# Weight-block sums of the convolution's quads: on VectorE while they are used, or in DRAM beforehand

## The chip, the cores and the metric

One core of one Trainium2 chip runs the whole program. The metric is the device time of one execution in microseconds, taken as the median of several runs. Beside these there is one profiled execution, whose span and instruction times are what the views of the profile show.

## What is computed

A trunk of two layers on a sequence of 512 tokens with 1024 features, all in float32. Cut to what matters here:

```python
def short_conv_mixer(x, w_in, w_conv, w_out):     # w_in: 1024 x 3072
    proj = x @ w_in
    bgate, cgate, xh = jnp.split(proj, 3, axis=-1)
    u = cgate * xh
    conv = causal_depthwise_conv(u, w_conv)       # width 3
    return (bgate * conv) @ w_out

def sqrelu_mlp(x, w_up, w_down):                  # 1024 -> 4096 -> 1024
    h = jax.nn.relu(x @ w_up)
    return (h * h) @ w_down

for i in range(2):
    x = x + rms_norm(mixer_i(rms_norm(x)))        # i = 0: mLSTM, i = 1: short_conv_mixer
    x = x + rms_norm(sqrelu_mlp(rms_norm(x)))
```

So the order of the work is mLSTM mixer, first MLP, convolution mixer, second MLP.

## The kernel before, in words

**Matmuls.** Float32 products are made from float32r halves: `split` (L79 to L84) writes the rounded half with a cast on ScalarE (ACT, L80) and the rest with a subtraction on VectorE (DVE, L81), and `mm3` (L112 to L117) issues three matmuls on TensorE (PE) for each pair of operands.

**Quads.** The products with `w_up` and with the convolution's `w_in` are made in pieces called quads. A quad takes two column blocks of 256 columns of the weights, so with the two halves of the 1024 rows it has four weight blocks of 512 x 256: a and b in the upper half, c and d in the lower one. In place of eight block products it makes seven, by the Strassen-Winograd scheme: each of the seven multiplies one combination of weight blocks by one combination of activation blocks. The activation side (`a11`, `a12`, `a22`, `p1`, `n2`, `r3`, `p4`) is made once for each layer in the class `Seven` (L199). The weight side is a, c, d and four sums: a+b, b+d, a+b+d and a+b+c+d. Before the change each quad loads its four blocks and makes the four sums with `tensor_tensor` additions on DVE. `Quad.block` (L814) is a load of 512 KB into a buffer called `raw` on the SyncE queue (SP), `Quad.factor` (L823) is the split of one weight operand, `prod` (L793) is one of the seven products, 24 matmuls of 256 columns.

**Three ways through a quad.** `enter` (L935) begins the first three quads of a layer early (products with a and c), while the layer before ends, and has the first quad's four sums made by `sums` (L849, additions on L852, L855, L856, L858). `run_first` (L861) finishes quad 0. `run` (L887) does the others; its four additions are L899, L905, L920 and L931. The convolution has six quads: four that give the gated value (`gated`, L1025) and two for the output gate (`out_gate`, L1064), run in the order 0, 1, 3, 2, 4, 5 (L1078 to L1080). Each MLP has eight.

**Buffers.** `raw` has 7 buffers, `u` (split weights, activations, residual) 15, the PSUM tiles `pu` 4 and `pd` 2. A load on SP waits until its `raw` buffer is released, that is, until the last DVE instruction that reads the buffer's former tile. In the convolution the value `u` of each gated quad takes a `raw` buffer as well, from a memset on GpSimd (POOL, L1036) to the last L1053.

**The end of a layer.** `last_product` (L280) makes the product with the last 1024 rows of `w_down`, or the whole product with `w_out`: two row tiles at a time in the two `pd` banks. `done` (L303) reads a finished bank with ACT (L181) and with DVE (L315 after a mixer, L318 after an MLP), and the next product in that bank waits for them. POOL makes a small power (L173) for each norm and, after an MLP, the product with the gain (L321). Between the last products `ahead` starts the next layer's `enter`.

**Queues.** SP carries all weight loads, in program order. POOL's queue carries the saving of the residual (`xd<-u`, L785), its loading again (`u<-xd`, L776, from `fetch_x`), gains (L160), the powers and the memsets, in program order too. A scheduler sets the order on each engine from the program and its own costs. In the first MLP each of the quads 2 to 7 is preceded by `down(g)` (L979), the product with one eighth of `w_down`; its results are added to `ys` by DVE (L1004, for g = 0 copied by ACT, L1002).

Of the kernel before, what the change touches and what calls it, by code (L numbers as in the profile page):

```python
# [8 lines left out]
F32 = mybir.dt.float32  # L9
# [5 lines left out]
P = 128  # L15
# [24 lines left out]
def tile_hybrid_trunk(  # L40
# [239 lines left out]
    def last_product(wm, r0, hT, g, tail, accs=None, ends=False, ahead=None):  # L280
# [61 lines left out]
        for t in range(2, NT):  # L342
            if ahead is not None:
                ahead()
            for cs in parts[t]:
                o = pd()
                ks(o, t, cs, 0, KO)
                done(o, t, cs)

# [404 lines left out]

    def scores_and_core(t):
        scores(t)
        if t > 0:
            core(t - 1, 0)
# [47 lines left out]
    class Quad:  # L806
# [3 lines left out]
        def __init__(self, wm, c0, c1, xT, take, claim=lambda: None):  # L810
            self.wm, self.cols, self.xT, self.take = wm, (c0, c1), xT, take
            self.claim = claim

# [47 lines left out]
        def run_first(self):  # L861
# [5 lines left out]
            f4, f5, f6, f7, f3 = (self.factor(t) for t in self.ts)  # L867
# [19 lines left out]
        def run(self, begun):  # L887
# [4 lines left out]
            bank = pd if begun else pu  # L892
            self.claim()
            a, b = self.block(0, 0), self.block(0, 1)
            if not begun:
                self.f1 = self.factor(a)
                self.begin(pu)
            y = self.y
            tt(out=a, in0=a, in1=b, op=ALU.add)  # L899
            f5 = self.factor(a)  # L900
# [3 lines left out]
            d = self.block(1, 1)  # L904
            tt(out=a, in0=a, in1=d, op=ALU.add)  # L905
            f6 = self.factor(a)
# [8 lines left out]
            c = self.block(1, 0)  # L915
# [4 lines left out]
            tt(out=b, in0=b, in1=d, op=ALU.add)  # L920
            prod(y, self.factor(b), f["r3"], False)
            o = bank()
            nc.scalar.mul(by_tile(o), by_tile(y), -1.0)
            prod(z, self.factor(d), f["p4"], False)
# [6 lines left out]
            tt(out=a, in0=a, in1=c, op=ALU.add)  # L931
            prod(o, self.factor(a), f["a22"], False)
            self.take(0, 1, self.values(), by_tile(o))

    def enter(quads):  # L935
# [7 lines left out]
        quads[0].sums()  # L943
# [12 lines left out]
    def mlp(i, xT, gain_of, tail_of, ends=False, ahead=None):  # L956
# [4 lines left out]
        def quad(g):  # L961
# [13 lines left out]
            return Quad(w_up[i], g * 512, g * 512 + 256, xT, take)  # L975
# [3 lines left out]
        def down(g):  # L979
            if g == 0:  # L980
                ys.extend(token_tiles())
            for hf, cs in enumerate(halves()):
# [6 lines left out]
                for t in range(NT):  # L989
# [11 lines left out]
                    if g == 0:  # L1001
                        nc.scalar.copy(yh, o)  # L1002
                    else:
                        nc.vector.tensor_tensor(out=yh, in0=yh, in1=o, op=ALU.add)  # L1004

# [13 lines left out]
    def conv(xT, gain_of, tail_of, ahead):  # L1019
# [5 lines left out]
        def gated(p):  # L1025
# [36 lines left out]
            return Quad(wm, D + p * 256, 2 * D + p * 256, xT, take, claim)  # L1062

        def out_gate(b):  # L1064
# [8 lines left out]
            return Quad(wm, b * 512, b * 512 + 256, xT, take)  # L1073
# [54 lines left out]
```

## Time and profile before

| | |
|---|---|
| median of 3 runs | 1108.53 us (1106.28 to 1109.0) |
| the profiled execution: its time | 1111.46 us |
| its span | 1109.7 us |
| its mean granted TensorE clock | 0.994 |
| first MLP, steady part, PE time | about 283 to 531 us |
| convolution, quads, PE time | 578.7 to 706.7 us |
| convolution, last product, PE time | 706.7 to 741.5 us |

How to read the views. The page gives the busy time of each engine over the span. The view of stretches gives, for each stretch of time, the busy time of each engine with its number of instructions, the granted TensorE clock as a share, the busy share of the 16 DMA engines and what they moved. Matmuls are pipelined and their ends are modelled, so PE can look busy while it runs below its rate; matmuls per microsecond say more. The view of waits gives for an engine and a line what it waited for, the sum in us, how often, and the longest. The view of groups gives count, busy time and mean duration of instructions of one line, then the idle time before them. The timeline gives start, duration, engine, line, operands and, in brackets, idle time before an instruction and what ended it. The DMA view gives packets and busy share of each queue, and for each kind of transfer its size and the median time from issue to landing.

### The profile page before, as it was taken

To read this page: it belongs to the slowest core of one execution; us is meant where nothing else is said; L and a number is where in the kernel's file an instruction comes from. 1 tells how busy PE (TensorE), PEld (TensorE's weight loads), DVE (VectorE), ACT (ScalarE), POOL (GpSimd) and SP (SyncE) were. 2 spreads that over 40 slices of the span, in tenths; PEclk is the share of its full clock that TensorE was granted. 3 is DMA by queue.
4 is the path that set the end of the run, shared out by engine and by line. 5 is a ranking of instruction groups with operands and counts; after the bars stand their busy time and mean duration, and the time that the engine had idled before them with its cause. 6 is when DMAs were issued, how large, how long until landed. Compare 5 with 4: busy or idle time off the path is not lost. (4 is left out here: it accounts for less than half of the span.)

```text
span 1109.7 us, 16027 instructions
## 1 busy us (share of the span) xinstructions
PE 1080.6 (97%) x6531; PEld 951.8 (86%) x6531; DVE 758.5 (68%) x1008; ACT 503.8 (45%) x780; POOL 70.3 (6%) x114
## 2 busy tenths in 40 slices
PE   7999999999999999999999999899999999999997
PEld 5878887789899899899879999778989989989986
DVE  5561567489776775758579998848967667575843
ACT  6441445365554244335346545636554434424521
POOL 1100010110000000000231000011000000000011
PEclk9999999999999999999999999989999999999999
DMA  8420264136344133163424362623533413415201
GB/s 266 134 76 1 76 228 138 71 102 198 117 135 134 46 126 125 47 208 110 144 89 153 95 209 96 200 105 104 182 117 128 135 56 114 133 44 203 96 19 57
DMA packets 104783, 133.73 MB, mean 121 GB/s; under 512 B 5221, under 2 KB 76165, under 8 KB 104710
## 3 DMA queue, kind: packets, MB, share of 16 engines
q1 hardware_dynamic: 100246, 116.46, 33.3%
q0 software_dynamic: 4464, 16.25, 4.0%
q8 instruction: 51, 0.84, 0.3%
q14 instruction: 22, 0.18, 0.1%
HBM read 124.31 MB, written 8.39 MB: 120 GB/s over the span
## 5 line engine op out<-in xcount | busy, mean ns | idle before, releaser
L81 DVE TENSOR_TENSOR u<-raw,u 128x1024 fp32r<-128x1024 f32 (+1 forms) x270 | 320.5, 1200 | 123.5 <-ACT u L80 123.1
L80 ACT CAST u<-raw 128x1024 fp32r<-128x1024 f32 (+1 forms) x270 | 272.3, 1028 | 216.2 <-PE pd L117 159.3
L115 PE MATMUL pu<-u 128*128 128x256 f32 (+1 forms) x1112 | 337.2, 303 | 3.5 <-ACT u L80 3.4
L116 PE MATMUL pu<-u 128*128 128x256 f32 (+1 forms) x1112 | 335.6, 302 | 0.8 <-DVE u L81 0.8
L117 PE MATMUL pu<-u 128*128 128x256 f32 (+1 forms) x1112 | 334.7, 301 | 0.8 <-DVE u L81 0.8
L115 PE MATMUL pd<-u,hb 128*128 128x512 f32 (+1 forms) x648 | 256.1, 395 | 5.5 <-DVE t L315 4.4
L116 PE MATMUL pd<-u,hb 128*128 128x512 f32 (+1 forms) x648 | 255.2, 394 | 0.0
L117 PE MATMUL pd<-u,hb 128*128 128x512 f32 (+1 forms) x648 | 255.1, 394 | 0.0
L115 PEld LDWEIGHTS pu<-u 128*128 128x128 f32 x1112 | 210.6, 189 | 13.7 <-ACT u L80 4.8
L116 PEld LDWEIGHTS pu<-u 128*128 128x128 f32 x1112 | 210.4, 189 | 10.1 <-DVE u L81 1.6
L117 PEld LDWEIGHTS pu<-u 128*128 128x128 f32 x1112 | 210.5, 189 | 9.6 <-DVE u L81 1.3
L115 PEld LDWEIGHTS pd<-u,hb 128*128 128x128 f32 x648 | 122.4, 189 | 35.2 <-DVE t L315 5.3
L117 PEld LDWEIGHTS pd<-u,hb 128*128 128x128 f32 x648 | 122.3, 189 | 28.2
L116 PEld LDWEIGHTS pd<-u,hb 128*128 128x128 f32 x648 | 122.5, 189 | 27.9 <-DVE u L81 0.6
L115 PE MATMUL pd<-u 128*128 128x256 f32 x312 | 88.3, 283 | 4.1 <-ACT pu L840 2.4
L116 PE MATMUL pd<-u 128*128 128x256 f32 x312 | 87.5, 281 | 0.0
L117 PE MATMUL pd<-u 128*128 128x256 f32 x312 | 87.3, 281 | 0.0
L1004 DVE TENSOR_TENSOR u<-u,pd 128x512 f32<-128x512 f32 x80 | 54.6, 683 | 36.8 <-PE pd L117 36.5
L181 ACT ACTIVATE junk<-u 128x512 bf16<-128x512 f32 (+1 forms) x49 | 30.5, 622 | 74.1 <-DVE u L318 53.3
L80 ACT CAST hb<-t 128x512 fp32r<-128x512 f32 x80 | 48.9, 619 | 32.5 <-DVE t L968 26.7
L115 PEld LDWEIGHTS pd<-u 128*128 128x128 f32 x312 | 58.8, 188 | 5.2 <-ACT pu L840 2.8
L116 PEld LDWEIGHTS pd<-u 128*128 128x128 f32 x312 | 58.8, 188 | 0.0
(173 smaller groups left out, 851.7 us busy)
## 6 DMA issues: line engine op xcount, KB each, us to landing
raw<-in_w_mlp_up_dram SPq DMA_DIRECT2D x76, 512.0 KB, 4.5
raw<-in_w_mlp_down_dram SPq DMA_DIRECT2D x64, 512.0 KB, 4.2
raw<-in_w_in_conv_dram SPq DMA_DIRECT2D x30, 512.0 KB, 4.8
raw<-in_w_in_mlstm_dram SPq DMA_DIRECT2D x24, 512.0 KB, 4.7
xd<-u POOLq DMA_DIRECT2D x12, 512.0 KB, 3.0
u<-xd POOLq DMA_DIRECT2D x12, 512.0 KB, 5.8
raw<-in_w_out_mlstm_dram SPq DMA_DIRECT2D x8, 512.0 KB, 4.1
raw<-in_w_out_conv_dram SPq DMA_DIRECT2D x8, 512.0 KB, 4.6
```

The lines of the kernel that those rows point to most:

```text
L80: hi = nc.scalar.copy(dst_hi, src)
L81: lo = nc.vector.tensor_tensor(out=dst_lo, in0=src, in1=dst_hi.bitcast(F32), op=ALU.subtract)
L115: nc.tensor.matmul(o, lh, rh, start=first, stop=False, skip_group_check=True)
L116: nc.tensor.matmul(o, lh, rl, start=False, stop=False, skip_group_check=True)
L117: nc.tensor.matmul(o, ll, rh, start=False, stop=last, skip_group_check=True)
L181: nc.scalar.activation(junk(n), src, AF.Square, scale=float(D) ** -0.5, accum_out=ms[:, i : i + 1])
L1004: nc.vector.tensor_tensor(out=yh, in0=yh, in1=o, op=ALU.add)
```

## The change

The four sums of all six quads of the convolution are made in DRAM during the first MLP. Two DRAM tensors hold them: `cx` for the four gated quads (four sums, 512 x 1024 each: the four quads' 256 columns lie side by side), `og` for the two output-gate quads (four sums, 512 x 2 x 256 each). A part is a range of rows of one tensor: four parts of 128 rows of `cx`, two of 256 rows of `og`, so that each transfer of a part has 512 KB. A part is nine transfers from POOL's queue. The first writes four elements from the tile `yh` that the MLP has just written, which only sets the part's place in time. Four plain copies fill the four sums with a, b, d and c. Then come four adding transfers: b onto the first sum, d onto the second, the first sum onto the third, the third onto the fourth. The third waits for the first, the fourth for the third. A part is recorded at the end of the first column half of each `down(g)`, g = 0 to 5, of the first MLP.

In the convolution each operand is now loaded as it stands, a sum by `sum_block`, a block by `block`: seven loads a quad, where there were four (six for a quad that is begun early). The additions on DVE go: 20 in the five `run` quads, 4 in `sums`. The MLPs are as before.

```diff
+    class Sums:
+        def __init__(self, name, wm, c0, c1, shape, key, quads):
+            self.all = dram.tile([4, 512] + shape, F32, name=name)
...
+            self.blocks = src(0, c0), src(0, c1), src(1, c0), src(1, c1)
...
+        def make(self, r0, r1, mark):
+            a, b, c, d = (blk[r0:r1] for blk in self.blocks)
+            f = [self.all[n, r0:r1] for n in range(4)]
+            first = self.all[:, r0]
+            first = first[:, 0, 0:1] if len(first.shape) > 2 else first[:, 0:1]
+            nc.gpsimd.dma_start(first, mark)
+            for dst, blk in zip(f, (a, b, d, c)):
+                nc.gpsimd.dma_start(dst, blk)
+            for dst, blk in list(zip(f, (b, d))) + [(f[2], f[0]), (f[3], f[2])]:
+                nc.gpsimd.dma_start(dst, blk, accum_op=ALU.add, max_dma_last_dim=D)
...
+    cx = Sums("cx", wc, D, 2 * D, [D], "conv", [D + p * 256 for p in range(4)])
+    og = Sums("og", wc, 0, 256, [2, 256], "conv", [0, 512])
+    later = [(cx, p * P, (p + 1) * P) for p in range(4)] + [(og, 0, 256), (og, 256, 512)]
...
+        def sum_block(self, i):
+            raw = raw_tile([4, 256])
+            nc.sync.dma_start(raw, self.pre[i])
+            return raw
...
-            f4, f5, f6, f7, f3 = (self.factor(t) for t in self.ts)
+            if self.pre is None:
+                f4, f5, f6, f7, f3 = (self.factor(t) for t in self.ts)
+            else:
+                f4, f5, f6, f7 = (self.factor(self.sum_block(i)) for i in (3, 0, 2, 1))
+                f3 = self.factor(self.block(1, 1))
...
-            tt(out=a, in0=a, in1=b, op=ALU.add)
-            f5 = self.factor(a)
+            if not pre:
+                tt(out=a, in0=a, in1=b, op=ALU.add)
+            f5 = self.factor(self.sum_block(0) if pre else a)
...
-        quads[0].sums()
+        if quads[0].pre is None:
+            quads[0].sums()
...
+                if i == 0 and hf == 0 and later:
+                    sm, r0, r1 = later.pop(0)
+                    sm.make(r0, r1, yh[0:4, 0:1])
```

Three places show what this does to the order. The first is POOL's queue during the first MLP. Before, from the last gain of the mLSTM layer's end to the first MLP's last product, it holds only the four loads of the residual (`xd` is the residual in DRAM, `u` its place in SBUF):

```order
L160 DMA gain<-in_norm_g_dram 128x1024
L776 DMA u<-xd_1452 128x1024
L776 DMA u<-xd_1453 128x1024
L776 DMA u<-xd_1454 128x1024
L776 DMA u<-xd_1455 128x1024
L321 TENSOR_TENSOR u<-u,gain 128x512 x3
```

Now, the fourth part of `cx`, the first of `og`, the residual's loads, and the beginning of the last part:

```order
L379 DMA cx<-u 4x1
L381 DMA cx<-in_w_in_conv_dram 128x1024 x4
L383 DMA cx<-in_w_in_conv_dram 128x4x256 x2
L383 DMA cx<-cx 512x256 x2
L379 DMA og<-u 4x1
L381 DMA og<-in_w_in_conv_dram 512x1x256 x4
L383 DMA og<-in_w_in_conv_dram 512x1x256 x2
L383 DMA og<-og 512x256 x2
L818 DMA u<-xd_1454 128x1024
L818 DMA u<-xd_1455 128x1024
L818 DMA u<-xd_1456 128x1024
L818 DMA u<-xd_1457 128x1024
```

Fifty-four transfers now stand between that gain and the L321 of the last product, the residual's loads behind five of the six parts and ahead of the sixth. The plain copies of `cx` go in rows of 1024 elements, all adding transfers in rows of 256.

The second place is DVE where the first MLP ends and the convolution begins (`raw` holds loaded weights, `pd` the last product's banks, `pt` transposed activations). Before:

```order
L81 TENSOR_TENSOR u_4929<-raw_4927,u_4929 128x1024
L852 TENSOR_TENSOR raw_4932<-raw_4932,raw_4934 128x1024
L855 TENSOR_TENSOR raw_4939<-raw_4932,raw_4937 128x1024
L856 TENSOR_TENSOR raw_4934<-raw_4934,raw_4937 128x1024
L81 TENSOR_TENSOR u_5012<-pt_5005,u_5012 128x4x128
L318 TENSOR_TENSOR u_2465<-u_2465,pd_4975 128x512
L858 TENSOR_TENSOR raw_4942<-raw_4942,raw_4939 128x1024
```

Now:

```order
L81 TENSOR_TENSOR u_4985<-raw_4983,u_4985 128x1024
L318 TENSOR_TENSOR u_2467<-u_2467,pd_5018 128x512
L168 SCALAR_TENSOR_TENSOR small_5079<-small_5013 128x1
L81 TENSOR_TENSOR u_5055<-pt_5048,u_5055 128x4x128
L274 SCALAR_TENSOR_TENSOR u_4270<-u_2467,small_5079,u_4270 128x512 x2
```

The release of the last product's last bank (L318) comes right behind the split of a loaded block, with no addition ahead of it.

The third place is DVE where the convolution's last product begins (`hb` holds the gated result in halves, `u_6511` and the like weights of `w_out` and of the next MLP). Before:

```order
L81 TENSOR_TENSOR hb_6381<-t2_6285,hb_6381 128x512
L81 TENSOR_TENSOR hb_6319<-t2_6416,hb_6319 128x512
L81 TENSOR_TENSOR u_6511<-raw_6509,u_6511 128x1024
L81 TENSOR_TENSOR u_6516<-raw_6514,u_6516 128x1024
L81 TENSOR_TENSOR u_6521<-raw_6519,u_6521 128x1024
L81 TENSOR_TENSOR u_6620<-raw_6618,u_6620 128x1024
L81 TENSOR_TENSOR u_6625<-raw_6623,u_6625 128x1024
L81 TENSOR_TENSOR u_6630<-raw_6628,u_6630 128x1024
L315 TENSOR_TENSOR t2_6489<-pd_6444,gain_6420 128x512
```

Now:

```order
L81 TENSOR_TENSOR u_6675<-raw_6673,u_6675 128x1024
L81 TENSOR_TENSOR hb_6435<-t2_6336,hb_6435 128x512
L81 TENSOR_TENSOR hb_6370<-t2_6471,hb_6370 128x512
L81 TENSOR_TENSOR u_6680<-raw_6678,u_6680 128x1024
L81 TENSOR_TENSOR u_6685<-raw_6683,u_6685 128x1024
L315 TENSOR_TENSOR t2_6544<-pd_6499,gain_6475 128x512
```

Between the last split of the gated result and the first read of a finished bank (L315) there were six splits of weights, and there are two.

More of the change, by code (lines that the diff above doesn't have):

```diff
@@ L892, in run @@
             bank = pd if begun else pu
+            pre = self.pre is not None
             self.claim()
[L894 removed]
+            if not pre:
+                a, b = self.block(0, 0), self.block(0, 1)
             if not begun:
[L896 removed]
+                self.f1 = self.factor(self.block(0, 0) if pre else a)
                 self.begin(pu)
             y = self.y
[L899 to L900 removed]
+            if not pre:
+                tt(out=a, in0=a, in1=b, op=ALU.add)
+            f5 = self.factor(self.sum_block(0) if pre else a)
             z = bank()
@@ L903, in run @@
                 prod(z, f5, f["p1"], True)
-            d = self.block(1, 1)
-            tt(out=a, in0=a, in1=d, op=ALU.add)
-            f6 = self.factor(a)
+            if not pre:
+                d = self.block(1, 1)
+                tt(out=a, in0=a, in1=d, op=ALU.add)
+            f6 = self.factor(self.sum_block(2) if pre else a)
             prod(y, f6, f["n2"], False)
@@ L914, in run @@
                 nc.scalar.copy(s2, by_tile(y))
-            c = self.block(1, 0)
+            if not pre or not begun:
+                c = self.block(1, 0)
             if not begun:
@@ L919, in run @@
                 self.take(0, 0, self.values(), by_tile(self.x))
-            tt(out=b, in0=b, in1=d, op=ALU.add)
-            prod(y, self.factor(b), f["r3"], False)
+            if not pre:
+                tt(out=b, in0=b, in1=d, op=ALU.add)
+            prod(y, self.factor(self.sum_block(1) if pre else b), f["r3"], False)
             o = bank()
             nc.scalar.mul(by_tile(o), by_tile(y), -1.0)
-            prod(z, self.factor(d), f["p4"], False)
+            prod(z, self.factor(self.block(1, 1) if pre else d), f["p4"], False)
             tt(out=s5, in0=by_tile(y), in1=s5, op=ALU.add)
@@ L930, in run @@
                 self.take(0, 0, self.v, None)
-            tt(out=a, in0=a, in1=c, op=ALU.add)
-            prod(o, self.factor(a), f["a22"], False)
+            if not pre:
+                tt(out=a, in0=a, in1=c, op=ALU.add)
+            prod(o, self.factor(self.sum_block(3) if pre else a), f["a22"], False)
             self.take(0, 1, self.values(), by_tile(o))
@@ L973, in take @@
                 split(hs[j][:, 0, half], hs[j][:, 1, half], c)
-            return Quad(w_up[i], g * 512, g * 512 + 256, xT, take)
+            return Quad(w_up[i], g * 512, g * 512 + 256, xT, take, i)
         ys = []
@@ L1060, in take @@
                         )
-            return Quad(wm, D + p * 256, 2 * D + p * 256, xT, take, claim)
+            return Quad(wm, D + p * 256, 2 * D + p * 256, xT, take, "conv", claim)
         def out_gate(b):
```

19 lines of the change are left out of this document (17 added, 2 removed).

## The prediction

> **What bounds the kernel now.** I read the page first, for the engines:
>
> ```profile
> span 1109.7 us, 16027 instructions
> PE 1080.6 (97%) x6531; PEld 951.8 (86%) x6531; DVE 758.5 (68%) x1008; ACT 503.8 (45%) x780; POOL 70.3 (6%) x114
> ```
>
> PE bounds nearly everything, so only time that PE loses can be won. A busy share hides such time, so I counted matmuls in stretches: one quad of the first MLP, the convolution's quads, the first MLP's last product, the convolution's, and two short ones inside the convolution.
>
> ```profile
> core 0: us, PE busy (x) PEld busy (x) DVE busy (x) ACT busy (x) POOL busy (x), PEclk, DMA share, GB/s
> 343.10:363.00 19.90, 19.90 (x170) 19.89 (x169) 13.94 (x16) 10.92 (x14) 0.00 (x0) 1.00 0.57 178
> 578.70:706.70 128.00, 122.41 (x1019) 121.41 (x1018) 117.21 (x137) 74.53 (x103) 7.23 (x16) 0.99 0.46 150
> 706.70:741.50 34.80, 30.58 (x123) 24.27 (x122) 19.16 (x27) 11.11 (x23) 3.05 (x6) 0.90 0.40 132
> 531.20:559.10 27.90, 27.90 (x122) 22.45 (x121) 13.87 (x21) 7.87 (x17) 6.99 (x8) 1.00 0.36 114
> 668.50:676.60 8.10, 5.89 (x34) 5.48 (x33) 6.75 (x6) 4.83 (x6) 0.00 (x0) 0.79 0.35 107
> 717.50:727.60 10.10, 5.88 (x16) 4.30 (x15) 5.25 (x6) 0.69 (x2) 0.00 (x0) 0.66 0.79 259
> ```
>
> An undisturbed quad runs 170 matmuls in 19.9 us, 0.117 us each. The convolution's 1019 would need 119.2 us so and take 128.0: **8.8 us lost**. Its last product takes 34.8 us where the MLP's, of the same size, takes 27.9: **6.9 us lost**. DVE is busy for 117.2 of the 128 us there, 92%, against 70% in the MLP's quad. The view of PE's waits from 570 to 760 us says who holds PE up:
>
> ```profile
> PE pd L115 <- DVE t L315: 4.2, 1, 4.2
> PE pu L115 <- ACT u L80: 2.2, 2, 1.8
> PE pt L261 <- DVE t L252: 1.3, 1, 1.3
> PE pd L115 <- DVE u L318: 1.3, 1, 1.3
> PE pu L117 <- DVE u L81: 0.8, 1, 0.8
> ```
>
> These are 9.8 us, four of the five on DVE. The ACT one waits for splits whose sum was late on DVE, as the timeline shows, first DVE, then ACT:
>
> ```profile
> 668.26 1.22 DVE L905 TENSOR_TENSOR raw<-raw 128x1024 f32<-128x1024 f32 x1
> 669.57 3.90 ACT L80 CAST u<-raw 128x1024 fp32r<-128x1024 f32 x4
> ```
>  The rest of the 15.7 us is PE running slowly after a wait: the granted clock is 0.79 around 670 us and 0.66 around 720. From 668.5, 34 matmuls at 0.117 us are 4.0 us and take 8.1, though the waits there sum to 2.2. The Trainium skill (TensorE: Matmul & The Clock Gate, Part 1) has the clock drop only after an idle window of some 3.4 us; here a wait of 1.8 us at most was followed by 0.79, so the measurement decides. By the rule that place would lose its 2.2 us alone, and the sum below would be 1.9 us smaller.
>
> **What goes.** The additions, from the view of groups (594 to 707 us for the first four, all of the program for the fifth):
>
> ```profile
> L899 DVE TENSOR_TENSOR raw<-raw 128x1024 f32<-128x1024 f32 x5 | 6.1, 1221 | 0.3 <-DMA raw<-in_w_in_conv_dram 0.2
> L920 DVE TENSOR_TENSOR raw<-raw 128x1024 f32<-128x1024 f32 x5 | 6.1, 1218 | 0.6 <-DMA raw<-in_w_in_conv_dram 0.6
> L905 DVE TENSOR_TENSOR raw<-raw 128x1024 f32<-128x1024 f32 x5 | 6.1, 1217 | 0.0
> L931 DVE TENSOR_TENSOR raw<-raw 128x1024 f32<-128x1024 f32 x5 | 6.1, 1215 | 0.0
> L852 DVE TENSOR_TENSOR raw<-raw 128x1024 f32<-128x1024 f32 x3 | 3.7, 1217 | 0.0
> ```
>
> That is 24.4 us in the `run` quads and 4 x 1.2 = 4.9 us in `sums`, 29.3 us of DVE. Left are 117.2 - 29.3 = 87.9 us of DVE in a stretch of 119, 74%, nearly the share at which the MLP's quads run without a wait. Each of the five waits has its own reason to go. DVE at the beginning:
>
> ```profile
> 579.48 1.22 DVE L855 TENSOR_TENSOR raw<-raw 128x1024 f32<-128x1024 f32 x1
> 580.62 1.22 DVE L856 TENSOR_TENSOR raw<-raw 128x1024 f32<-128x1024 f32 x1
> 581.76 0.68 DVE L81 TENSOR_TENSOR u<-pt,u 128x512 fp32r<-128x512 f32 x1
> 582.36 0.68 DVE L318 TENSOR_TENSOR u<-u,pd 128x512 f32<-128x512 f32 x1
> ```
>
> L318 and, through it, the norm and L252 of the last token tile stand behind the additions; they come 3.7 us (three additions) to 4.9 us (four) earlier. And at the last product:
>
> ```profile
> 713.45 1.30 DVE L81 TENSOR_TENSOR hb<-t,hb 128x512 fp32r<-128x512 f32 x2 [2.88 <-ACT hb L80]
> 714.66 6.89 DVE L81 TENSOR_TENSOR u<-raw,u 128x1024 fp32r<-128x1024 f32 x6
> 721.47 1.28 DVE L315 TENSOR_TENSOR t<-pd,gain 128x512 f32<-128x512 f32 x2
> ```
>
> Six late splits, 6.9 us, stand between the gated result and L315. In the new order there are two, 2.4 us: L315 would begin 4.5 us earlier, at 717.0, where PE ran dry at 717.6.
>
> What is late next is the chain at the layer's start: at the second MLP's start PE's longest wait is on ACT's L840, 1.2 us (first row below). I leave 1.5 us for it, between nothing and this 1.2 plus a restart at a lower clock. So the convolution wins 15.7 - 1.5 = **14.2 us**; if only waits and no clock came back, 9.8 - 1.5 = 8.3.
>
> ```profile
> PE pd L115 <- ACT pu L840: 1.2, 1, 1.2
> DMA to landing us min/median/max: 3.5/4.8/7.0
> ```
>
> **More loads in the convolution.** 42 in place of 30, each of 512 KB; the second row is the landing of those of before. SP passes twelve more of them ahead of the loads of `w_out`. A `raw` buffer turns over in at most 7.0 us of landing, 1.0 of cast (3.90 for four, above) and 1.2 of subtraction (6.89 for six), 9.2 us; with five of seven buffers (two for gated values) that is one operand in 1.8 us, and PE takes one in 24 x 0.117 = 2.8. At 7 x 0.52 MB in 19.9 us they move 184 GB/s, and the quad of the first MLP quoted above had 178. Hidden: 0 us; without this cover a wait like the 1.8 us one returns now and then.
>
> **The parts in DRAM.** No adding transfer and no DRAM to DRAM copy is in the trace. What must hold is that POOL is free when it is needed and that weights still arrive. The relevant rows: what writes the tiles that mark the first and the sixth part, the first use of the residual in the last product, POOL's first work there, the landings of the residual's loads (four of 512 KB in a row), and one of their neighbours, the loads of `w_up` from 283 to 531 us.
>
> ```profile
> 295.99 0.59 ACT L1002 COPY u<-pd 128x512 f32<-128x512 f32 x1
> 501.13 0.68 DVE L1004 TENSOR_TENSOR u<-u,pd 128x512 f32<-128x512 f32 x1
> 551.58 1.41 DVE L274 SCALAR_TENSOR_TENSOR u<-u,small 128x512 f32<-128x512 f32 x2 [1.74 <-POOL small L173]
> 542.68 1.29 POOL L321 TENSOR_TENSOR u<-u,gain 128x512 f32<-128x512 f32 x1 [63.27 <-ACT junk L181]
> DMA to landing us min/median/max: 3.5/5.8/8.2
> raw<-in_w_mlp_up_dram SPq DMA_DIRECT2D x20, 512.0 KB, 4.5
> xd<-u POOLq DMA_DIRECT2D x12, 512.0 KB, 3.0
> ```
>
> POOL's queue holds a part until the third addition has landed and the fourth is issued: the mark (3.0, the small end of POOL's stores), the four copies (8.2), the first two additions together, the third. It has 542.7 - 501.8 = 40.9 us for the sixth part, and as much between the earlier ones (one `down` and one quad, 42 us). If an addition costs what a load does, 4.5 for one and 5.8 for two, a part holds POOL for 21.5 us. If one costs 8.2 and two 16.4, as if it moved four loads' bytes, 35.8. Both fit; I take the middle, 29, and 0 us for the end. The Trainium skill (Collectives: The Full Stack, The bandwidth ceiling) says that an adding transfer reads two sources through one ring and so runs at half a copy's rate; an estimate by that lies inside these bounds; no run here shows it. Behind a waiting part stand the residual's loads, not used before that L274, and the next part's mark: DVE writes the marked tile again one `down` later, and if the mark is still to come, L1004 waits for it and PE's `pd` bank for L1004. The weights' cover: a load issued at 344.19 us is first cast at 360.20.
>
> ```profile
> 344.19 7.92 SPq L817 DMA_DIRECT2D raw<-in_w_mlp_up_dram  x4
> 360.20 1.05 ACT L80 CAST u<-raw 128x1024 fp32r<-128x1024 f32 x1
> ```
>
> 16 us for a landing of 4.5: it may grow by a factor of 3.5. Nothing is charged, and the rival has the price. A reason for a gain in the first MLP I see none.
>
> **Sum.** On the profiled execution's time, 1111.46 - 14.2 = 1097.3 us. The median of the runs, 1108.53, lies 2.9 below that execution, so **1094 us** as a median. From no change a measurement of this kernel can tell about 0.3%, 3.3 us.
>
> **Rivals.**
>
> *POOL is late (slower).* The adding transfers go in rows of 256 elements, 512 to a transfer, not in the long rows of the copies. If each row is a slow read, add and write, one addition takes A and two take 2A, and a part holds POOL for 11.2 + 3A. It decides at A = 9.9 us; from there the parts pile up, the sixth ending at 296.6 + 6 x (11.2 + 3A), where the first mark stands at 296.6. With A = 11.6, twice the 5.8, that is 572.6: L321, and with it norms and the next layer, 29.9 us late. 1094 + 30 = **1124 us**. For it: no row shows an addition. Against it: it needs twice what any 512 KB transfer here took on the median.
>
> *Weights starve (about even or slower).* Copies and additions share the 16 engines with the weights. Should a load take 19 us in place of 4.5, it comes 3 us past its 16, once a part: 6 x 3 = 18 us, 1094 + 18 = **1112 us**; at 17 us it is 6 us and 1100. For it: SP's loads come in bursts, 178 GB/s in the quad above. Against it: the engines' share there is 0.57. The Trainium skill (DMA: Bandwidth & Descriptors, Queues, rings and completion order) has each DMA engine alternate between queues packet by packet; by that the larger packets of POOL's copies would take more than half. No run here shows it.
>
> *Half of it.* The last product's stall stays, since ACT still casts three blocks of the next MLP ahead of the last gated result: in the row at 713.45 DVE sat 2.88 us for ACT. Then 6.9 us are not won, **1101 us**. Against it: those casts waited for buffers that a late DVE held.
>
> **Chances.** The forecast 0.56, half of it 0.10, weights starve 0.13 (0.02 of it still faster, 0.05 even, 0.06 slower), POOL late 0.20, new waits in the convolution that eat the gain 0.01, even. That makes faster 0.68, same 0.06, slower 0.26. Below, 1090 is all 15.7 us won, 1092.8, and a run as far below the median as the lowest of the three, 2.3 us. Above, 1124 takes in starving and the late POOL up to A = 11.6; beyond it lies most of what is left of its 0.20. The likeliest case alone is 1090 to 1100, its upper end being waits won and no clock.
>
> **What would show it.** Right: in the convolution's stretch DVE near 75%, PE's waits on L315, L318, L252 and L80 gone, the last product near 28 us with a clock of 1.00; in the first MLP 170 matmuls in 19.9 us as before and L321 near 542 us. Wrong: POOL's L321 late behind an adding transfer, or PE waiting on casts that waited for DMA between 296 and 531 us, or additions that take 10 us and more.

## The result and the profile after

The changed kernel takes **1099.22 us**, the median of five executions (1098.73 to 1101.50), against 1106.28 us (1104.65 to 1109.00) for the kernel before on the same chip. The ratio is 0.9937, with a 95% interval of 0.9916 to 0.9958: faster, by more than the 0.3% that can be told from no change. The forecast was 1094 in a range of 1090 to 1124. The profiled execution took 1098.78 us, 12.7 us less than the profiled one of before (1111.46), for which 14.2 were forecast.

In the kernel after, line numbers from the new class on are higher: L888 is the negation that was L840, L895 the copy of a bank to SBUF (`put_by`), L1064 the former L1004. The page's engine row first:

```profile
PE 1076.3 (98%) x6531; PEld 948.6 (86%) x6531; DVE 733.4 (67%) x984; ACT 503.6 (46%) x780; POOL 116.6 (11%) x168
```

DVE has 25.1 us and 24 instructions less, POOL 54 instructions more, the transfers of the six parts. The next view is that of stretches: one quad of the first MLP, the whole of the time in which parts are made, the convolution's quads (which end 6 us earlier), its last product, and the two short ones inside the convolution.

```profile
core 0: us, PE busy (x) PEld busy (x) DVE busy (x) ACT busy (x) POOL busy (x), PEclk, DMA share, GB/s
343.10:363.00 19.90, 19.90 (x170) 19.87 (x169) 13.94 (x16) 10.92 (x14) 3.33 (x3) 1.00 1.09 274
283.00:531.00 248.00, 247.20 (x1534) 220.93 (x1535) 169.48 (x192) 106.75 (x136) 48.70 (x58) 1.00 0.81 214
578.99:701.00 122.01, 120.91 (x1021) 120.30 (x1020) 97.12 (x117) 77.67 (x107) 6.95 (x15) 1.00 0.69 222
701.00:729.30 28.30, 28.20 (x123) 22.47 (x122) 13.87 (x23) 7.85 (x20) 3.04 (x6) 1.00 0.32 105
717.50:727.60 10.10, 10.10 (x45) 8.17 (x44) 5.52 (x11) 3.09 (x9) 2.25 (x4) 1.00 0.14 54
668.50:676.60 8.10, 8.10 (x71) 8.10 (x70) 4.21 (x4) 4.33 (x6) 0.00 (x0) 1.00 0.75 229
```

The same matmuls take 122.0 us where they took 128.0, and the last product 28.3 where it took 34.8. Where the clock was 0.79 and 0.66 it is 1.00: 71 matmuls in 8.1 us for 34, and 45 in 10.1 for 16. The first MLP's quad has its 170 matmuls in 19.9 us as before, though the 16 DMA engines' share rose from 0.57 to 1.09. For the whole stretch of the parts the row of the kernel before is this one:

```profile
283.00:531.00 248.00, 247.39 (x1536) 221.01 (x1536) 169.97 (x193) 109.09 (x139) 2.10 (x4) 1.00 0.36 117
```

PE's busy time there differs by 0.2 us, while the DMA share went from 0.36 to 0.81. PE's waits from 570 to 760 us, in the kernel after (us in total, times, longest):

```profile
PE pd L115 <- ACT pu L888: 1.2, 1, 1.2
PE pd L115 <- ACT t L895: 1.0, 1, 1.0
PE pd L115 <- DVE t L315: 0.2, 1, 0.2
```

Of the 9.8 us, the five waits on L315, L80, L252, L318 and L81, 0.2 us is left. The first row is the chain at the next layer's start, which the prediction had named; it is as long as before. The second is new: at 597 us ACT sits for a load, and PE for the copy behind it. Rows of the timeline, one of ACT and then POOL's, say how the loads and the parts stand:

```profile
597.01 1.05 ACT L80 CAST u<-raw 128x1024 fp32r<-128x1024 f32 x1 [2.64 <-DMA raw<-in_w_in_conv_dram]
...
502.20 0.53 POOL L379 DMA_DIRECT2D og<-u  x1 [9.79 <-DVE u L1064]
...
508.99 1.35 POOL L383 DMA_DIRECT2D og<-in_w_in_conv_dram  x1 [1.28 <-DMA og<-in_w_in_conv_dram]
...
518.08 1.03 POOL L383 DMA_DIRECT2D og<-og  x1 [5.47 <-DMA og<-in_w_in_conv_dram]
529.98 1.03 POOL L383 DMA_DIRECT2D og<-og  x1 [10.87 <-DMA og<-og]
543.30 2.54 POOL L321 TENSOR_TENSOR u<-u,gain 128x512 f32<-128x512 f32 x2 [12.29 <-ACT junk L181]
```

The sixth part holds POOL from 502.20 to 531.0, 28.8 us. L321 then begins at 543.30 (542.68 before), after 12.29 us in which POOL was idle, and what releases it is ACT, not an addition. The DMA issues from 283 to 531 us (number, KB each, median us to landing), and then the additions alone:

```profile
raw<-in_w_mlp_up_dram SPq DMA_DIRECT2D x20, 512.0 KB, 10.3
cx<-cx POOLq DMA_DIRECT2D x8, 512.0 KB, 9.3
...
DMA to landing us min/median/max: 5.3/9.6/14.2
```

A load of `w_up` lands in 10.3 us on the median instead of 4.5, and an addition in 9.6 (9.3 for `cx<-cx`, 10.0 for `og<-og`).

### The profile page after: what moved, and what is told of

The parts are those of the page before. It is cut to its first block, busy times and chain, and to the rows that moved or that the text cites. A ratio compares the mean times of both kernels' runs of the same rounds, so it can differ in the third digit from the quotient of the medians.

```text
span 1097.1 us, 16129 instructions
## 1 busy us (share of the span) xinstructions
PE 1076.3 (98%) x6531; PEld 948.6 (86%) x6531; DVE 733.4 (67%) x984; ACT 503.6 (46%) x780; POOL 116.6 (11%) x168
## 3 DMA queue, kind: packets, MB, share of 16 engines
q1 hardware_dynamic: 106582, 122.75, 35.1%
## 5 line engine op out<-in xcount | busy, mean ns | idle before, releaser
L81 DVE TENSOR_TENSOR u<-raw,u 128x1024 fp32r<-128x1024 f32 (+1 forms) x270 | 321.0, 1200 | 134.8 <-ACT u L80 134.3
L80 ACT CAST u<-raw 128x1024 fp32r<-128x1024 f32 (+1 forms) x270 | 273.2, 1028 | 208.7 <-PE pd L117 159.4
L117 PE MATMUL pu<-u 128*128 128x256 f32 (+1 forms) x1112 | 334.3, 301 | 0.0
L117 PE MATMUL pd<-u,hb 128*128 128x512 f32 (+1 forms) x648 | 254.1, 392 | 0.0
L115 PEld LDWEIGHTS pu<-u 128*128 128x128 f32 x1112 | 210.1, 189 | 10.5 <-ACT u L80 1.4
L117 PEld LDWEIGHTS pu<-u 128*128 128x128 f32 x1112 | 209.9, 189 | 8.6 <-DVE u L81 0.3
L117 PEld LDWEIGHTS pd<-u,hb 128*128 128x128 f32 x648 | 121.7, 188 | 28.0
L117 PE MATMUL pd<-u 128*128 128x256 f32 x312 | 87.2, 281 | 0.0
L1064 DVE TENSOR_TENSOR u<-u,pd 128x512 f32<-128x512 f32 x80 | 54.6, 683 | 36.6 <-PE pd L117 36.5
L181 ACT ACTIVATE junk<-u 128x512 bf16<-128x512 f32 (+1 forms) x49 | 30.5, 622 | 76.8 <-DVE u L318 54.5
L80 ACT CAST hb<-t 128x512 fp32r<-128x512 f32 x80 | 49.0, 619 | 32.5 <-DVE t L1028 26.6
```

The lines of the kernel that those rows point to most:

```text
L80: hi = nc.scalar.copy(dst_hi, src)
L81: lo = nc.vector.tensor_tensor(out=dst_lo, in0=src, in1=dst_hi.bitcast(F32), op=ALU.subtract)
L115: nc.tensor.matmul(o, lh, rh, start=first, stop=False, skip_group_check=True)
L117: nc.tensor.matmul(o, ll, rh, start=False, stop=last, skip_group_check=True)
L181: nc.scalar.activation(junk(n), src, AF.Square, scale=float(D) ** -0.5, accum_out=ms[:, i : i + 1])
```

## The experiments

**Theory A**: the waits that went were DVE's, and the parts are hidden, so that the gain is what the waits and the clock behind them cost. **Rival B**: the parts cost something in the first MLP, which eats a part of the gain. Behind these stands the question why the median fell by 7.1 us where the two profiled executions differ by 12.7.

### b_again: the kernel before once more

No edit.

> The kernel before, unchanged, for more executions of it. Theory A (the two profiled executions differ by 12.7 us but the medians by 7.1 because executions of the kernel before differ among themselves: how long PE runs at a lower granted clock after its waits changes from one to the next): times between 1104 and 1111 us, and a time falls as the granted clock rises from 0.994 towards 0.998; in this execution's profile the convolution's last product takes less than the 34.8 us of the first profile, or its quads less than 128.0. Rival B (the waits of before are the same each time, and the medians differ less because the kernel after loses time in its first MLP in most executions): clock 0.994 and the same 128.0 and 34.8 us again, times near 1106.

Measured: 1108.31 us, median of 12 executions (1103.78 to 1110.81); ratio 1.0004 (0.9990 to 1.0017). Its profiled execution took 1107.78 us, with these waits from 570 to 760 us, and these stretches:

```profile
PE pd L115 <- DVE t L315: 3.6, 2, 3.3
PE pu L115 <- ACT u L80: 2.4, 2, 2.0
PE pt L261 <- DVE t L252: 1.5, 1, 1.5
PE pd L115 <- DVE u L318: 1.3, 1, 1.3
PE pu L117 <- DVE u L81: 0.4, 1, 0.4
```

```profile
706.70:741.50 34.80, 31.48 (x141) 25.30 (x139) 22.00 (x32) 13.05 (x28) 3.39 (x6) 1.00 0.42 145
668.50:676.60 8.10, 5.91 (x34) 5.69 (x35) 6.32 (x6) 4.90 (x7) 0.00 (x0) 0.79 0.42 129
717.50:727.60 10.10, 6.78 (x30) 5.37 (x29) 4.05 (x5) 1.35 (x4) 0.00 (x0) 1.00 0.75 250
```

The waits are the same five, 9.2 us. But behind the longest of them the clock is 1.00, where the first profile had 0.66. At 668 us it is 0.79 as there. So the waits belong to the kernel, and how much clock is lost behind them differs from one execution to the next.

### plain_loads: no parts, plain blocks in place of the sums

The quads load a plain block where they would load a sum, and no sum is made; so the sums of weight blocks are left out of the computation, and everything after DVE's additions is as in the kernel after.

```diff
-            raw = raw_tile([4, 256])
-            nc.sync.dma_start(raw, self.pre[i])
-            return raw
+            kh, nh = ((0, 0), (1, 1), (0, 1), (1, 0))[i]
+            return self.block(kh, nh)
...
-                if i == 0 and hf == 0 and later:
+                if False:
```

> Leaves out the sums: no parts are made in DRAM, and the convolution loads a plain block where it would load a sum, seven loads a quad and no additions. Theory A: the parts in DRAM are hidden, so this takes what the kernel after takes, 1099 us within 2. Rival B: the parts cost some 5 us in the first MLP, so this takes 1094 us.

Measured: 1098.46 us (1097.42 to 1098.97); ratio 0.9917 (0.9903 to 0.9931). The interval overlaps that of the kernel after, 0.9916 to 0.9958. The first MLP's stretch is that of the kernel before again:

```profile
283.00:531.00 248.00, 247.38 (x1536) 221.12 (x1537) 170.00 (x193) 108.96 (x139) 2.10 (x4) 1.00 0.36 117
```

Without parts PE gets 247.38 us there, with them 247.20. The new wait, on the copy that is L894 in this kernel, stays, 1.7 us, so the parts don't cause it.

### parts_only: the parts are made and not used

```diff
-            self.pre = made.get((key, c0))
+            self.pre = None
```

> Makes all six parts in DRAM but uses none of them: the convolution adds on VectorE as before. Theory A: the time of the kernel before, 1106 us within 2, with loads of the first MLP that land in 10 us in place of 4.5 and nobody who waits for them. Rival B: slower than before by some 5 us, 1111.

Measured: ratio 1.0010 (0.9994 to 1.0026). Eleven of the twelve executions took 1105.47 to 1113.77 us, 1108.71 on the median, beside 1107.91 for the kernel before; one took 2731.19 us, stands outside the ratio, and has no explanation here. (With it the median is 1109.02.) The parts cost nothing that can be measured; the interval allows 2.9 us at most. The profiled execution took 1105.47 us. The stretch of the parts loses nothing, and the waits of before are all back (from 283 to 760 us):

```profile
283.00:531.00 248.00, 247.34 (x1536) 221.12 (x1537) 169.82 (x193) 106.68 (x136) 47.81 (x58) 1.00 0.81 212
668.50:676.60 8.10, 5.89 (x48) 5.52 (x46) 6.50 (x6) 5.47 (x7) 0.00 (x0) 1.00 0.40 120
717.50:727.60 10.10, 8.88 (x38) 7.25 (x39) 3.32 (x7) 0.69 (x2) 0.56 (x1) 1.00 0.57 187
```

```profile
PE pd L115 <- DVE t L315: 2.7, 2, 2.5
PE pu L115 <- ACT u L80: 2.2, 2, 1.8
PE pt L261 <- DVE t L252: 1.4, 1, 1.4
PE pd L115 <- DVE u L318: 1.3, 1, 1.3
...
PE pu L117 <- DVE u L81: 0.3, 1, 0.3
```

These are 7.9 us, and here the clock is 1.00 behind all of them. With this run and the one before it, B's 5 us fall.

### rows_4k: the additions in longer rows

```diff
-                nc.gpsimd.dma_start(dst, blk, accum_op=ALU.add, max_dma_last_dim=D)
+                nc.gpsimd.dma_start(dst, blk, accum_op=ALU.add, max_dma_last_dim=4 * D)
```

> The adding transfers in rows of 1024 elements in place of 256. If an addition's time goes by its bytes, it still lands in about 9 us, and a part still holds POOL for some 29 us. If it goes by its rows, it lands in well under 7 us and a part holds POOL for some 22 us. The time is 1099 us within 2 either way, as the parts are hidden (theory A); by rival B it falls by 1 to 3 us when the parts get shorter.

Measured: 1100.14 us (1098.81 to 1103.30); ratio 0.9938 (0.9921 to 0.9955), no different from the kernel after. The landing of the additions and one wait of PE from 283 to 760 us:

```profile
DMA to landing us min/median/max: 5.4/8.4/11.8
...
PE pd L115 <- DVE u L318: 1.6, 1, 1.6
```

Rows four times as long make an addition 1.2 us faster on the median, between what was expected by bytes and by rows, and hidden. The wait on L318, at 541 us, is not in the kernel after's profile; it comes back below.

### first_four and last_two: which additions made which wait

All six parts are made in both. In first_four the last two of the six quads in the order of work add on DVE as before, in last_two the first four do.

```diff
-            self.pre = made.get((key, c0))
+            self.pre = made.get((key, c0)) if c0 not in (D + 768, 512) else None
```

> All six parts are made, but only the first four of the convolution's six quads read their sums from DRAM; the last two quads add on DVE as before (9.8 us of additions in the last 40 us of the stretch). Theory A (DVE's backlog builds up over the whole stretch; each wait goes when DVE has slack ahead of it): the waits at 581, 592 and 648 us go, the one of 2.1 us at 668 us shrinks to under 1 us since DVE comes to it without a backlog, and of the 3.5 us wait in the last product some 2 us or less stays: 1099 to 1102 us. Rival B (the waits at 668 us and in the last product come from the additions of the last two quads alone): both stay whole (2.1 and 3.5 us), and only about 3 us of the gain is there: 1104 to 1106 us.

```diff
-            self.pre = made.get((key, c0))
+            self.pre = made.get((key, c0)) if c0 in (D + 768, 512) else None
```

> The complement: all six parts are made, but only the last two of the six quads read their sums from DRAM; the first four add on DVE as before. Theory A: the waits at 581, 592 and 648 us stay (3.6 us together), those at 668 us (2.7 us) and in the last product (3.5 us) go or shrink to under 1 us: 1101 to 1103 us. Rival B (waits come from the additions in the same quads alone): the same three waits stay and the same two go; it differs from A only in the sum with the complement: by B the two gains add up to the whole gain of some 8 us, by A they add up to more.

Measured, against 1108.97 us of the kernel before beside them: first_four 1098.43 us (1097.76 to 1099.17), ratio 0.9905 (0.9892 to 0.9919); last_two 1100.22 us (1099.64 to 1101.73), ratio 0.9927 (0.9914 to 0.9941). Each alone has nearly the whole gain, 10.5 and 8.8 us, so the two gains add up to far more than the full change wins. Both came out a little below the times that were expected. The last product in first_four, and then the quads in last_two:

```profile
706.70:741.50 34.80, 34.65 (x158) 27.93 (x157) 19.79 (x32) 14.06 (x31) 3.95 (x7) 1.00 0.32 106
```

```profile
578.70:706.70 128.00, 125.05 (x1035) 123.41 (x1035) 118.34 (x140) 79.66 (x108) 7.25 (x16) 1.00 0.61 196
```

In first_four the last two quads' additions are all there, and the last product still has no gap. So its stall was not made by those additions alone. But two things differ from the kernel before there. DVE is done with the gated result earlier, at 707.32 us where it was 714.66, and three splits of weights stand ahead of L315 where there were six:

```profile
707.32 3.49 DVE L81 TENSOR_TENSOR u<-raw,u 128x1024 fp32r<-128x1024 f32 x3
711.93 0.69 DVE L315 TENSOR_TENSOR t<-pd,gain 128x512 f32<-128x512 f32 x1 [1.12 <-ACT junk L181]
```

L315 waits here for ACT's read of the finished bank. With six splits, 6.8 us, ahead of it, it would have begun at 714.1 us, some 2 us late. So the run doesn't tell a lag of DVE from the order of its work: the scheduler orders each version anew. At 668 us the order changed as well. There PE waited for a sum that L905 added behind four L1053 (667 us); in first_four the same addition, L961, begins at 657.38 us, ahead of them.

In last_two DVE is as busy as ever, 118.3 of 128 us, and the waits at 668 us and in the last product are gone with the additions near them; those at 581 and 592 us stay (1.3 us each by the view of waits). Two splits stand ahead of L315 there. Rival B of these two, under which each quad makes its own waits, falls.

### og_twice: POOL made late

The fifth and the sixth part are each made twice, with the same values.

```diff
                     sm.make(r0, r1, yh[0:4, 0:1])
+                    if sm is og:
+                        sm.make(r0, r1, yh[0:4, 0:1])
```

> The last two of the six parts are each made twice, with the same values, so that POOL is busy with parts until about 578 us, and the two multiplications of the first MLP's last product on POOL (L321) come some 35 us later than at 543 us. This is the prediction's rival of the late POOL, forced. Theory A (the parts are hidden only because POOL is done before the last product): the time grows by about what L321 is late beyond the 1 us or less of slack it has, 30 to 36 us: 1129 to 1136 us, with one PE wait of 30 us or more between 545 and 600 us. Rival: PE finds other work, or the late step has slack that the profile does not show: under 10 us, 1099 to 1109 us.

Measured: 1139.00 us (1138.12 to 1140.83); ratio 1.0273 (1.0259 to 1.0288). POOL's L321 and PE's waits:

```profile
586.31 4.07 POOL L321 TENSOR_TENSOR u<-u,gain 128x512 f32<-128x512 f32 x3
...
PE pt L261 <- DVE t L252: 32.6, 1, 32.6
...
594.90:630.00 35.10, 34.09 (x194) 29.48 (x195) 26.76 (x42) 22.23 (x46) 14.07 (x18) 0.92 0.31 108
```

L321 comes 43.0 us later than in the kernel after, and the kernel is 39.8 us slower, 3 us more than the upper end of what was expected. PE waits 32.6 us for the norm behind L321, some 4 us more than in the kernel after at other places, and then has a clock of 0.92 for 35.1 us, 2.8 us more.

### sixth_twice: POOL a little late

```diff
                     sm.make(r0, r1, yh[0:4, 0:1])
+                    if sm is og and r0 == 256:
+                        sm.make(r0, r1, yh[0:4, 0:1])
```

> All parts are made and used, the sixth twice with the same values, so that POOL is busy with it until about 560 us and L321 comes some 15 us later than at 543 us. When the fifth was doubled too, L321 came 43.1 us later and PE waited 32.8 us for L252 behind it, so 10.3 us were slack. Theory A with that slack: PE waits 15 - 10.3, about 5 us, before 567 us, and the time is 1103 to 1106 us. Rival (the prediction's price, each us that L321 is late costs one): 1113 to 1116 us. Second rival (the wait comes from transfers that crowd out the loads, not from POOL): over 1106 us with PE waits on ACT's casts that wait for DMA.

Measured: 1114.95 us (1111.73 to 1115.64); ratio 1.0049 (1.0034 to 1.0064). L321 and PE's waits:

```profile
561.58 4.07 POOL L321 TENSOR_TENSOR u<-u,gain 128x512 f32<-128x512 f32 x3
...
570.21 1.97 PE L261 MATMUL pt<-ident,t 128*128 128x128 f32 x8 [11.38 <-DVE t L252]
...
PE pt L261 <- ACT raw L218: 1.7, 2, 1.6
...
570.20:600.00 29.80, 28.07 (x152) 24.00 (x153) 21.46 (x34) 17.00 (x38) 13.28 (x16) 0.94 0.34 118
```

My expectation from the slack failed, and the prediction's price held: 18.3 us later, 15.7 us slower. PE runs out of work at 558.8 us here (570.21 less the wait of 11.38), and at 562.3 in og_twice. PE starts again 8.6 us after L321 begins (561.58 to 570.21). So L321 may begin at 550.2, and the slack is 6.9 us; I had worked it out from a run in which PE itself was 3.5 us late. Of 18.3 us, 11.4 are left, which is PE's wait. Another 1.7 us goes to ACT, and 1.8 us to a clock of 0.94 in 29.8 us.

### f3_first: the new wait

In the first quad, the plain block is loaded ahead of the last sum.

```diff
-                f4, f5, f6, f7 = (self.factor(self.sum_block(i)) for i in (3, 0, 2, 1))
-                f3 = self.factor(self.block(1, 1))
+                f4, f5, f6 = (self.factor(self.sum_block(i)) for i in (3, 0, 2))
+                f3 = self.factor(self.block(1, 1))
+                f7 = self.factor(self.sum_block(1))
```

> The changed kernel with one pair of loads in another order in the first quad: the plain block (its fourth transfer) is loaded and split ahead of the last sum, as the product with it comes ahead of the product with that sum. Theory A: the new PE wait of 1.2 us at 597 us (behind an ACT cast that waits 2.6 us for that block's load) goes, and no other comes: 1097.5 to 1098.5 us. Rival: the wait only moves to the last sum, whose load is now the late one: 1099 us, with a wait of about 1 us near 600 us.

Measured: 1100.12 us (1098.50 to 1101.12); ratio 0.9918 (0.9906 to 0.9931). Nothing was won: the wait is still there, and one on L318 joins it, as in rows_4k.

```profile
PE pd L115 <- ACT t L895: 1.6, 1, 1.6
...
598.24 1.04 ACT L80 CAST u<-raw 128x1024 fp32r<-128x1024 f32 x1 [3.19 <-PE pu L117]
599.19 0.58 ACT L895 COPY t<-pd 128x512 f32<-128x512 f32 x1
```

But its cause is another one. In the kernel after, the quad's fifth load is issued at 590.90 us, when the first of the loaded sums has been split, and comes 2.64 us late for its cast. In f3_first the cast in that place waits for PE: PE's last L117 ahead of the gap begins at 597.96, and the cast at 598.24. What both have in common is that L895, the copy that PE needs, stands behind this cast on ACT. The copy ahead of the cast would be the next thing to try; it wasn't run. The wait on L318 is 1.2 us.

### cx_only and og_only: fewer parts

Only the four parts for the gated values, or only the two for the out gate; the other quads add on DVE.

```diff
-    later = [(cx, p * P, (p + 1) * P) for p in range(4)] + [(og, 0, 256), (og, 256, 512)]
+    later = [(cx, p * P, (p + 1) * P) for p in range(4)]
...
-            self.pre = made.get((key, c0))
+            self.pre = made.get((key, c0)) if c0 >= D else None
```

> Only the four parts of cx are made (until about 445 us), for the four quads of gated values; the two quads of the out gate add on DVE as before. Theory A: no wait of the convolution comes back, since DVE keeps a third of the relief in every pair of quads, and the sixth part no longer delays the loads at 525 to 536 us, so the wait of 1.2 to 1.7 us at 541 us that some executions of the kernels with all six parts show is gone too: 1097 to 1098.5 us. Rival (the out gate's additions come back as waits at 668 us or in the last product): 1101 to 1105 us.

```diff
-    later = [(cx, p * P, (p + 1) * P) for p in range(4)] + [(og, 0, 256), (og, 256, 512)]
+    later = [(og, 0, 256), (og, 256, 512)]
...
-            self.pre = made.get((key, c0))
+            self.pre = made.get((key, c0)) if c0 < D else None
```

> The complement: only the two parts of og are made, during the first two groups of the first MLP (until about 360 us), for the two quads of the out gate, the third and the sixth in the order of work; the four quads of gated values add on DVE as before. Theory A (a third of the relief is enough from the third quad on): the waits at 581 and 592 us stay, 2.9 us, that at 648 us and those at 668 us (2.7 us) and in the last product (3.5 us) go: 1100 to 1102 us. Rival (the fifth quad's own additions make the wait at 668 us): 2.7 us more and a lower clock behind it, 1103 to 1106 us.

Measured, against 1108.66 us of the kernel before beside them: cx_only 1098.40 us (1098.09 to 1100.31), ratio 0.9909 (0.9895 to 0.9923); og_only 1099.39 us (1098.85 to 1099.51), ratio 0.9913 (0.9898 to 0.9928). Neither can be told from the kernel after. cx_only took what was expected. In og_only the waits on L252 and L318 stay, 1.3 us each, and the others go, as expected; the time is 0.6 us under the one forecast. It needs 18 transfers in place of 54 and takes a third of the additions from DVE; its quads:

```profile
578.70:706.70 128.00, 125.38 (x1039) 123.89 (x1039) 119.04 (x141) 80.06 (x109) 7.25 (x16) 1.00 0.62 197
```

### first_one: one quad's additions

All parts are made; only the first quad uses its sums.

```diff
-            self.pre = made.get((key, c0))
+            self.pre = made.get((key, c0)) if c0 == D else None
```

> All six parts are made, but only the first quad reads its sums from DRAM; the other five add on DVE (24.4 us of additions). Theory A with the head start lost (DVE idles between the first quad and the fifth, so the 4.9 us don't carry): the waits at 581 and 592 us go, those at 648 and 668 us and in the last product stay: 1104 to 1106 us. Theory A with the head start kept: only the last product's wait comes back in part: 1099 to 1102 us.

Measured: 1101.12 us (1100.84 to 1101.32); ratio 0.9930 (0.9917 to 0.9942). Four additions, 4.9 us of DVE at the stretch's beginning, win about 7.5 of the 10 us that the best version wins. The waits at 648 and 668 us are gone too, and of the last product's stall 1.5 us are left, with five splits ahead of L315:

```profile
708.14 5.76 DVE L81 TENSOR_TENSOR u<-raw,u 128x1024 fp32r<-128x1024 f32 x5
713.82 1.28 DVE L315 TENSOR_TENSOR t<-pd,gain 128x512 f32<-128x512 f32 x2
```

At 668 us DVE comes to the four L1053 (L1116 here) at 665.22 us, hardly earlier than before (665.62). But the sum that PE waits for is added ahead of them, at 661.69, and no longer behind them. So here too a head start and another order came together.

## Why the prediction was right, and what was off in its size

**The waits that go.** Right, each of them: 9.8 us on L315, L80, L252, L318 and L81 became 0.2. L318 and L252 stood behind the first quad's additions, as the prediction read it: first_four and first_one, which take these away, don't have the two waits, and last_two and og_only, which keep them, have 1.3 us of each. For the last product the prediction counted six splits ahead of L315, and two in the new order. That count is borne out. In the table, the room is the time from the end of DVE's last split of the gated result to the moment when L315 could begin, 0.72 us after ACT begins to read the bank (L181), as it does where it waits for ACT alone; the splits are those that DVE makes in between.

| kernel | room, us | splits | their time, us | L315 late by, us | PE's longest wait on L315, us |
|---|---|---|---|---|---|
| before | 2.7 | 6 | 6.8 | 4.1 | 4.2 |
| b_again | 3.6 | 6 | 6.8 | 3.2 | 3.3 |
| parts_only | 4.5 | 6 | 6.8 | 2.4 | 2.5 |
| first_one | 4.5 | 5 | 5.7 | 1.2 | 1.3 |
| first_four | 4.6 | 3 | 3.4 | 0 | none |
| after | 6.3 | 2 | 2.3 | 0 | 0.2 |

parts_only, first_one and first_four have the same room, and the number of splits sets the wait. With two splits even the room of before, 2.7 us, would have been enough; with six even that of the kernel after, 6.3 us, would not quite. So the order of DVE's work accounts for this stall at least as well as its load. No run keeps the additions and changes the order alone, so how the gain at 668 us and in the last product divides between the two stays open.

DVE's share in the quads fell to 80% (97.1 of 122.0 us), not to 74%. The 29.3 us were a sum of durations; DVE's busy time over the program fell by 25.1, 20.1 of them in the quads and 5.3 in the last product (19.2 to 13.9). The share itself was no sign of what would happen: in og_only and last_two DVE is busy for 118 to 119 of 128 us, over 92% as before, and the long stalls are gone.

**The clock.** Here is the term that was mis-sized. The prediction took 15.7 us as lost, of which 9.8 were waits and the other 5.9 a lower clock, and then set the median of the kernel after 2.9 us below its profiled execution, as before's lay. Both rest on one execution of before that was unusually slow: 1111.46 us. None of the 53 executions of before that ran beside the experiments took over 1110.82. Their times go with the granted clock:

| clock of the execution | executions of before | mean, us |
|---|---|---|
| 0.994 | 9 | 1110.5 |
| 0.995 to 0.997 | 37 | 1108.2 |
| 0.998 | 7 | 1105.8 |

The kernel after, whose waits are 1.2 us at most, ran at 0.997 to 0.999 in all five executions, and its profiled execution is 0.4 us below its median. So the offset of 2.9 us had no counterpart, and that is the larger part of the 5.2 us between 1094 and 1099.22. An execution with a clock of 1.00 behind the stalls at 668 us and in the last product shows what the waits alone are worth: that of parts_only, 1105.47 us, with 7.9 us of waits on the five lines. The kernel after's, 1098.78 us, has 1.2 us on L895 and L315; the difference of the waits is 6.7 us, and that of the times too. The other 2.4 us, from 1105.8 to the median of the 53, 1108.18, are what a usual execution loses beside that, where 5.9 were taken. Not all of them need be clock: b_again's profiled execution took 2.3 us more than that of parts_only and had 1.3 us more of waits on the five lines.

The Trainium skill (TensorE: Matmul & The Clock Gate, Part 1) says that the window by which the clock is set runs freely, and that the same kernel meets it at another phase in each run. The runs agree: after a wait on L315 of 4.2 us the clock was 0.66, after one of 3.3 us 1.00, and after the waits at 668 us 0.79 twice and 1.00 once. Its figure for the idle time that lowers the clock, about 3.4 us, does not fit the two drops there, behind waits of 2.0 us at most, 2.2 and 2.4 us in sum.

**The residual.** 1.5 us were left for what is late next, by the chain at the layer's start. That chain did not grow: 1.2 us before and after. In its place stand 3.0 us in the stretches themselves: by the ends of the matmuls in the two traces, the quads went from 128.2 to 121.9 us, 6.3 for 8.8, and the last product from 34.9 to 28.5, 6.4 for 6.9. Of these 3.0, 1.2 is the new wait at 597 us (one matmul begins at 597.28 and the next at 598.60, where 0.12 is usual): the part on more loads charged 0 us and said that such a wait might return now and then, and it returns once, behind the first quad's fifth load. Most of the rest is pace: without the wait the quads take 120.7 us and not 119.2; why is not shown.

**The parts.** Right: 0 us. A part held POOL for 27 to 34 us, 29 were taken. L321 moved by 0.6 us. The additions were slower than the 4.5 to 8.2 us that I had as bounds: 9.6 us on the median, and 9.9 was the point from which POOL would be late by the prediction's sum; those of `og` reached 10.0, which the prediction had named as a sign of being wrong. By that sum a part would have held POOL for 40 of the 40.9 us that it has, which is close. It held it for less, since the first two additions of a part run side by side and don't take twice one's time: in the sixth part the third addition is issued 9.1 us after the first (508.99 to 518.08). The weights' loads took 10.3 us for 4.5, a factor of 2.3 where the cover was 3.5. The copies of the same 512 KB land in this:

```profile
DMA to landing us min/median/max: 4.2/7.3/9.2
```

The Trainium skill (Collectives: The Full Stack, The bandwidth ceiling) gives the adding transfers of a collective half a copy's rate. No run here tests that: an addition of a sum (`cx<-cx`) landed in 9.3 us on the median and copies, four at a time, in 7.3 each, but no copy was made alone.

**The rivals.** POOL late did not occur, but its price is measured: 43.0 us late cost 39.8, 18.3 cost 15.7. That is 1 us for 1 us less some 3 us, as the prediction had it without the slack of 6.9 us; in sixth_twice a lower clock and ACT take back 3.5 of them. Weights starving: no wait of PE on a load in the first MLP. The half of it: the stall of the last product went entirely, and first_one, which keeps 1.5 us of it, takes the 1101 us that this rival gave, by chance.

**What stays open.** rows_4k, f3_first and og_twice have a wait of 1.2 to 1.7 us on L318 at 541 to 544 us, which the kernel after's profile, cx_only, og_only and plain_loads don't have. The first three make the sixth part, whose additions share the DMA engines with the loads whose splits stand ahead of L318; but so do the kernel after, first_four, last_two, first_one and sixth_twice, without it. It may be the price of the sixth part in some executions; the runs don't settle it. None of the versions beats the change by more than the intervals allow.

## What to carry to other kernels

Where TensorE waits for an engine, look at what stands ahead of the awaited instruction in that engine's order, and not only at how busy the engine is: here DVE was busy for 92% in kernels with long stalls and in kernels without, and the stall of the last product went by how many splits stood ahead of L315. A version that takes away less work is scheduled anew too, and can win nearly as much: 18 transfers were enough here, and one quad's additions for three quarters. Try the smallest relief first, and a change of the order alone. Read a lost clock from several executions before it goes into a sum; the waits are the kernel's, the clock behind them is partly the execution's, and a kernel without the waits has little of it to lose. Spare DMA time under a stretch bound by TensorE can take adding transfers, as long as their queue has an end: POOL's next due work set the limit, and beyond it each us cost nearly one.

## What the runs showed of the hardware

- An adding transfer of 512 KB within DRAM landed in 5.3 to 14.2 us, beside weight loads at a DMA share of 0.81, and 4 KB rows in place of 1 KB rows brought the median from 9.6 to 8.4.
- With the parts' transfers beside them the DMA share went from 0.36 to 0.81, and the landing of the 512 KB loads of `w_up` from 4.5 to 10.3 us on the median.
- The issue of one addition of 512 KB in 1 KB rows held POOL for 1.35 us where the operand was a block of the weights (508.99), and for 1.03 where it was one of the sums (518.08 and 529.98).
- In one execution of the kernel before (b_again), TensorE's granted clock was 0.79 after two waits that sum to 2.4 us, and 1.00 after one of 3.3 us.
